# A two-layer mixture-of-experts trunk: full fp32 one-hot products, the router fed between two norms, the first token tile placed under the second

## The chip, the cores and the metric

The kernel runs on one core of one Trainium2 chip. The metric is the device time of one launch in microseconds (us), the median of several runs; less is better. The core's engines are named PE (TensorE, which multiplies matrices; PEld is its loading of weights), DVE (VectorE), ACT (ScalarE), POOL (GpSimd) and SP (SyncE, which here issues the weight transfers).

## The reference, cut to what matters

The input is 256 tokens of 1024 numbers, and there are two layers. In each layer `mod = silu(c) @ w_mod[l] + b_mod[l]` is split into six vectors of 1024: shift 1, scale 1, gate 1, shift 2, scale 2, gate 2 (`v` = 0 to 5 in the kernel).

```
h = layer_norm_plain(x) * (1 + sc1) + sh1
q, k, v, p = split(h @ w_in[l])
y = concat([attention(rope(q), rope(k), v), pool_mixer(p)]) @ w_out[l]
x = layer_norm_affine(alpha * x + g1 * y)
h = layer_norm_plain(x) * (1 + sc2) + sh2
scores = softmax(h @ w_router)
gates = top-2 experts inside the best of four groups, by scores + router_bias, weights normalised
y = sum over 16 experts e of gates[:, e] * (silu(h @ w_gate[e]) * (h @ w_up[e])) @ w_down[e]
x = layer_norm_affine(alpha * x + g2 * y)
```

Everything is float32. The weights are some 280 MB, and each is read once.

## The kernel before, in words

The tokens stand in two tiles of 128 (`t` = 0, 1). SP issues all weight transfers in one fixed order, the list `st` (class `Stream`), in pieces of 1 MB, into a ring of 21 buffers (`NS`); `st.allow(n)` says how many of them may hold weights, and `st.free` gives one back when PE has used it. The order of work on each engine is the order in which the code calls it; an engine does its instructions in that order.

A layer has these stages. The **entry** (`ready`, `enter`, `qk_mm`, the last loop of the file): the first scale and shift are multiplied out (`mod_mm`, `mod_fin`), the rows are normed, transposed, scaled and shifted, and multiplied with the query and key weights. The **mixer** (`mixer`): values, pooling, attention, and on DVE the sums over the weights of three other vectors (`mod_dve`, L361). The **routing**: `out_mm(t)` multiplies with `w_out` (L622), `norms_of(t)` adds the residual and does both norms on DVE, `turn(t)` transposes the normed rows (L653), `logits(t)` multiplies them with the router weights (L697), `exps(t)` finishes the softmax (L712 to L714), `router` chooses the experts for both tiles together on DVE (L782 to L810) and finds each token's place in its expert's batch of 64 slots (L816 to L824). `gate()` spreads gate 2 over the partitions (L347, L349). `warm(n)` are matrix products without use (L283), put where PE would stand idle. The **experts**: `onehot` writes a 0/1 matrix of token by slot, `gather(i)` multiplies the normed rows with it (L876), for four pairs of experts at a time (i = 0 and 4). Then for each of 8 pairs: `gate_up` (L918), `silu`, `act_t` (transposes, L941), `down` (L960), and `combine`, which adds the weighted rows back to their tokens through the transposed 0/1 matrix `STt` (L984).

In `gather` and `combine` a float32 operand is split into two of the type float32r: a rounded part and the rest (`xh`, `xl`; `oh`, `ol`). Each product is then made twice, once with each part:

```
for xs in (xh, xl):
    T.matmul(b, xs[:, t, k * 128:(k + 1) * 128], SX[i][t], start=(n == 0), stop=(n == 3))
```

DVE and ACT make the parts (L679, L725 to L727 for the rows; L973, L974 for the experts' results). Only the second half of the last pair's columns is combined by float32 products as they are (L980).

## Time and profile before

| | |
|---|---|
| time, median of 3 runs | 723.83 us (722.95 to 725.26) |
| time of the profiled execution | 724.93 us |
| its span, first to last instruction | 723.1 us |
| mean granted clock of PE | 0.986 of full speed |
| PE busy | 678.9 us, 94% of the span |
| DVE busy | 326.8 us, 45% |
| ACT busy | 124.8 us, 17% |
| moved by DMA | 280.37 MB, mean 388 GB/s |

The profile is of one execution. All its times count from the first instruction. A matrix product of float32 numbers leaves two MATMUL records, one of float32r or bfloat16 leaves one. A row of the timeline merges neighbours of one kind (x48 is 48 records), and what ended the idle time before it stands in brackets.

### The profile page before, as it was taken

What the parts mean: (1) busy time and instruction counts of PE and PEld (TensorE: products, weight loads), DVE (VectorE), ACT (ScalarE), POOL (GpSimd) and SP (SyncE); (2) the same over time, 40 slices, a digit from 0 to 9 for tenths busy, and PEclk for the clock granted to TensorE, in tenths of its full rate; (3) what the DMA queues carried; (4) which work ended last, traced back from release to release, by engine and by line L of the source; (5) the groups of instructions that cost most, each with busy time, mean ns of one, the idle gap of its engine ahead of it and who ended that gap; (6) DMA issues with size and microseconds to landing.
All of it is one profiled execution on the core that took longest, in us unless ns stands there. A gap on an engine that the chain in (4) does not pass through costs nothing. (4 is left out here: it accounts for less than half of the span.)

```text
span 723.1 us, 8334 instructions
## 1 busy us (share of the span) xinstructions
PE 678.9 (94%) x3213; PEld 316.8 (44%) x3218; DVE 326.8 (45%) x582; ACT 124.8 (17%) x268; POOL 49.7 (7%) x76
## 2 busy tenths in 40 slices
PE   5999899999999999989979999998999999998994
PEld 2447555553333533423324575555333344342331
DVE  4008897662332532413153966666323243241305
ACT  1011432130110210121002035213210011012100
POOL 5001501100000000000010051010000000000002
PEclk9999999999999999999989999999999999999998
DMA  9999999999999999999999999767699999999992
GB/s 307 366 384 409 408 409 420 373 421 392 424 420 420 422 421 421 420 416 418 395 406 392 409 410 406 310 272 301 282 420 422 421 424 419 420 422 418 418 395 77
DMA packets 61729, 280.37 MB, mean 388 GB/s; under 512 B 5008, under 2 KB 14264, under 8 KB 38632
## 3 DMA queue, kind: packets, MB, share of 16 engines
q1 hardware_dynamic: 61040, 279.20, 96.1%
q8 instruction: 30, 0.49, 0.3%
q10 hardware_dynamic: 312, 0.32, 0.1%
q0 software_dynamic: 320, 0.14, 0.1%
q14 instruction: 27, 0.22, 0.1%
HBM read 278.59 MB, written 1.05 MB: 387 GB/s over the span
## 5 line engine op out<-in xcount | busy, mean ns | idle before, releaser
L918 PE MATMUL ps<-wr 128*64 128x512 f32 x1024 | 226.1, 596 | 0.0
L918 PEld LDWEIGHTS ps<-wr 128*64 128x64 f32 x1024 | 73.5, 138 | 147.2 <-issue 142.3
L960 PE MATMUL ps<-wr,s 128*64 128x512 f32 x512 | 113.8, 595 | 3.7 <-DVE s L945 2.9
L960 PEld LDWEIGHTS ps<-wr,s 128*64 128x64 f32 x512 | 35.5, 137 | 72.0 <-issue 63.8
L970 DVE SCALAR_TENSOR_TENSOR s<-ps,gc,gb 128x512 f32<-128x512 f32 x32 | 24.0, 748 | 84.0 <-PE ps L960 84.0
L455 PE MATMUL ps<-wr,hT 128*128 128x512 f32 x128 | 57.0, 597 | 0.4 <-ACT hT L429 0.2
L361 DVE SCALAR_TENSOR_TENSOR wr<-wr,condT 128x1024 f32<-128x1024 f32 x42 | 55.8, 1329 | 2.3 <-DMA wr<-in_w_mod_dram 0.9
L622 PE MATMUL ps<-wr,hT 128*128 128x512 f32 (+1 forms) x160 | 55.7, 507 | 0.1
L389 POOL TENSOR_TENSOR rs<-rs,mhalf 128x1 f32<-128x1 f32 x16 | 13.2, 823 | 554.1 <-DVE rs L388 554.1
L935 DVE TENSOR_TENSOR s<-s,ps 128x512 f32<-128x512 f32 x16 | 11.0, 687 | 86.5 <-PE ps L918 86.5
L973 ACT CAST wr<-s 128x512 fp32r<-128x512 f32 x30 | 18.5, 618 | 164.7 <-PE ps L918 107.7
L974 DVE TENSOR_TENSOR wr<-s,wr 128x512 fp32r<-128x512 f32 x30 | 20.8, 692 | 55.6 <-ACT wr L973 55.6
L622 PEld LDWEIGHTS ps<-wr,hT 128*128 128x128 f32 x160 | 30.2, 190 | 23.8 <-issue 21.5
L455 PEld LDWEIGHTS ps<-wr,hT 128*128 128x128 f32 x128 | 23.6, 190 | 28.9 <-issue 27.1
L984 PE MATMUL ps<-wr,sT 128*128 128x512 f32 x120 | 33.6, 413 | 0.0
L578 PE MATMUL ps<-wr,hT 128*128 128x512 f32 x64 | 28.3, 595 | 0.0
L504 PE MATMUL ps<-hT,wr 128*128 128x256 f32 x128 | 28.1, 380 | 0.0
L984 PEld LDWEIGHTS ps<-wr,sT 128*128 128x128 f32 x120 | 20.9, 189 | 16.3 <-issue 13.0
L933 DVE SCALAR_TENSOR_TENSOR s<-s,ps 128x512 f32<-128x512 f32 x16 | 11.0, 685 | 36.7 <-ACT s L932 36.7
L504 PEld LDWEIGHTS ps<-hT,wr 128*128 128x128 f32 x128 | 24.2, 190 | 4.5 <-issue 1.3
L876 PE MATMUL ps<-s,xn 128*128 128x512 f32 x64 | 25.4, 398 | 0.3 <-DVE s L854 0.3
L996 DVE TENSOR_TENSOR xt<-xt,ps 128x512 f32<-128x512 f32 x40 | 25.2, 683 | 0.5
(240 smaller groups left out, 611.5 us busy)
## 6 DMA issues: line engine op xcount, KB each, us to landing
wr<-in_w_gate_dram SPq DMA_DIRECT2D x64, 1024.0 KB, 19.3
wr<-in_w_up_dram SPq DMA_DIRECT2D x60, 1024.0 KB, 19.3
wr<-in_w_down_dram SPq DMA_DIRECT2D x56, 1024.0 KB, 19.5
wr<-in_w_mod_dram SPq DMA_DIRECT2D x48, 1024.0 KB, 15.1
wr<-in_w_in_dram SPq DMA_DIRECT2D x16, 1024.0 KB, 15.1
wr<-in_w_out_dram SPq DMA_DIRECT2D x8, 1024.0 KB, 18.7
wr<-in_w_down_dram SPq DMA_DIRECT2D x12, 512.0 KB, 11.1
wr<-in_w_up_dram SPq DMA_DIRECT2D x8, 512.0 KB, 17.4
```

The source lines that it names most:

```text
L361: V.scalar_tensor_tensor(acc, w[:, kk], condT[:, k, 0:1], acc, op0=OP.mult, op1=OP.add)
L455: T.matmul(pq[t][n], hT[:, k, t * 128:(t + 1) * 128], w[:, kk, n * 512:(n + 1) * 512], start=(k == 0), stop=(k == 7))
L504: T.matmul(pp[g // 2][:, (g % 2) * 256:(g % 2) * 256 + 256], w[:, kk, g * 128:(g + 1) * 128], hT[:, k, :], start=(k == 0 and g % 2 == 0), ...
L578: T.matmul(pv[t], hT[:, k, t * 128:(t + 1) * 128], w[:, kk, :], start=(k == 0), stop=(k == 7))
L622: T.matmul(py[t][-1][:, 0:c1 - c0], catT[:, k, t * 128:(t + 1) * 128], w[:, kk, n * 512 + c0:n * 512 + c1], start=(q == 2 and kk == 0), st ...
L876: T.matmul(b, xs[:, t, k * 128:(k + 1) * 128], SX[i][t], start=(n == 0), stop=(n == 3))
L918: T.matmul(bs[nm][64 * j:64 * j + 64, :], XE[i][k // 4][:, k % 4, c0:c0 + 64], st.get((nm, l, 2 * i + j, q))[:, k - k0, :], start=(k == 0) ...
L960: T.matmul(bo[n][64 * j:64 * j + 64, :], AT[i][:, k, 64 * j:64 * j + 64], st.get(("d", l, 2 * i + j, q))[:, k - k0, (n - n0) * 512:(n - n0 ...
L970: V.scalar_tensor_tensor(o, bo[n], GC[i], g2[:, c0], op0=OP.mult, op1=OP.mult)
L974: V.tensor_sub(ol[:, c0], o, oh[:, c0].bitcast(F))
L984: T.matmul(b, STt[i][:, t * 128:(t + 1) * 128], o[:, n * 512:(n + 1) * 512], start=(start and j == 0), stop=(stop and j == 1), skip_group_ ...
L996: V.tensor_add(b if i == NPAIR - 3 else xt[:, t, c0], xt[:, t, c0], b)
```

## The change

Five things are changed.

1. `gather` and `combine` use float32 operands as they are, and each product is made once. The parts `xh`, `xl`, `oh`, `ol` and the instructions that make them go. The experts' results stand in the buffer `hT` instead of a slot of the ring for each pair, and two of the limits of `st.allow` are one higher.
2. The scale and shift of the second layer's entry (vectors 1 and 0) were multiplied out by vector: vector 1 in the first layer's routing, with its `mod_fin` in the second pair, vector 0 at the entry. Now it is by halves of the columns, both vectors at once (`mod1`): half 0 at the entry, half 1 between the query and key products, which go in four parts. The weights come in that order, behind the experts' weights.
3. `turn(t)` takes the rows between the two norms. The mean and the spread of the second norm are put in at the logits (two more instructions on DVE), from sums over the router weights that 16 products make (L749 in the new file, 8 before).
4. `out_mm` is cut in parts. The logits and the choice of experts for tile 0 (`route(0)`) and its places (`place(0)`) come between the parts for tile 1, and the gather's products with tile 0 for four of eight row blocks behind them. Tile 1 follows by itself: `turn(1)`, logits, `gate()`, softmax, `route(1)`, `place(1)`, then 12 products of the gather. Tile 1's second norm goes to ACT. Of the 10 products of `warm` in layer 0's routing and the 17 in layer 1's, two each stay.
5. In layer 0 the transposed queries are copied by ACT instead of DVE (L528).

```diff
-        if l + 1 < DEPTH:
-            add_mod(l + 1, 1)
         for i in range(NPAIR):
             add_pair(l, i)
         if l + 1 < DEPTH:
-            add_mod(l + 1, 0)
+            for q in range(4):
+                if q % 2 == 0:
+                    add_mod1(q // 2)
+                add_qk(l + 1, q)
...
+    def mod1(h):
+
+        acc = ps()
+        for k in range(8):
+            for v in range(2):
+                j = 2 * v + k % 2
+                T.matmul(acc[32 * j:32 * j + 32, :], condT[:, k, :], st.get(("m1", h, v, k // 4))[:, k % 4, :],
+                         start=(k < 2), stop=(k > 5))
+            if k % 4 == 3:
+                for v in range(2):
+                    st.free(("m1", h, v, k // 4))
...
+
             ready(0)
-            qk_mm(0)
+            enter(l, 0, 0, hT, xn)()
+            qk_mm(0, (0, 1))
+            part = mod1(1)
             ready(1)
+            enter(l, 1, 0, hT, xn)()
+            mod1_fin(1, part)
+            fins = [enter(l, 0, 1, hT, xn)]
+            qk_mm(1, (0, 1))
+            fins.append(enter(l, 1, 1, hT, xn))
+            for fin in fins:
+                fin()
+            qk_mm(0, (2, 3))
...
-                (A.copy if n else V.tensor_copy)(dst[:, :, t * 128:(t + 1) * 128], b.rearrange("p (c s) -> p c s", c=4))
+                (A.copy if n or not l else V.tensor_copy)(dst[:, :, t * 128:(t + 1) * 128], b.rearrange("p (c s) -> p c s", c=4))
...
+        def place(t):
+
+            pb = ps()
+            if t:
+                T.matmul(pb[:, 0:16], ones, M[:, 0], start=True, stop=False)
+            T.matmul(pb[:, 0:16], tri, M[:, t], start=not t, stop=True)
+            V.scalar_tensor_tensor(posm[:, t], M[:, t], -OFF, pb[:, 0:16], op0=OP.mult, op1=OP.add)
+            return onehot_t(posm, 0, t)
...
+        exps(0, logit_mm(0))
+        route(0)
+        out_mm(1, 1)
+        residual(1, 1)
+        out_mm(1, 2, (2, 3))
+        S0 = [place(0)]
+        out_mm(1, 2, (0, 1))
+        residual(1, 2)
+        first_norm(1)
+
+        gb0 = [ps() for _ in range(4)]
+        for k in range(4):
+            T.matmul(gb0[k], xn2[:, 0, k * 128:(k + 1) * 128], S0[0], start=True, stop=False)
...
         turn(1)
         logits(1)
-        exps(1)
-        return xh, xl, (mx, ex, sm), gate
+        pl = logit_mm(1)
+        gate()
+        st2[1] = mv, rs = stats(xt[:, 1])
+        exps(1, pl)
+
+        nb = tn([1], "r_nb")
+        V.scalar_tensor_tensor(nb, mv[:, 0:1], -1.0, rs, op0=OP.mult, op1=OP.mult)
+        o, i = in_rows(1)
+        A.activation(o, i, AF.Identity, scale=rs, bias=nb)
+        route(1)
+        warm(2)
+        S0.append(place(1))
...
+        def part_mm(b, i, k, t):
+            T.matmul(b, X[:, t, k * 128:(k + 1) * 128], SX[i][t], start=(t == 0), stop=(t == 1))
+
         def gather(i):
 
             halves = [slot().rearrange("p (k s) -> p k s", k=4) for _ in range(2)]
+            for j in range(4):
+                XE[i + j] = halves
             for k in range(8):
                 b = ps()
-                n = 0
                 for t in range(2):
-                    for xs in (xh, xl):
-                        T.matmul(b, xs[:, t, k * 128:(k + 1) * 128], SX[i][t], start=(n == 0), stop=(n == 3))
-                        n += 1
-                o = halves[k // 4][:, k % 4]
-                if k % 2:
-                    V.tensor_scalar(o, b, sc2[:, k:k + 1], sh2[:, k:k + 1], op0=OP.mult, op1=OP.add)
-                else:
-                    A.activation(o, b, AF.Identity, scale=sc2[:, k:k + 1], bias=sh2[:, k:k + 1])
+                    part_mm(b, i, k, t)
+                modulate(b, halves[k // 4][:, k % 4], k)
+
+        def gather_first():
+
+            halves = [slot().rearrange("p (k s) -> p k s", k=4) for _ in range(2)]
             for j in range(4):
-                XE[i + j] = halves
+                XE[j] = halves
+            bs = dict(enumerate(gb0))
+            for k in (4, 5):
+                bs[k] = ps()
+                part_mm(bs[k], 0, k, 0)
+            for k in range(8):
+                if k > 5:
+                    bs[k] = ps()
+                    part_mm(bs[k], 0, k, 0)
+                part_mm(bs[k], 0, k, 1)
+                modulate(bs[k], halves[k // 4][:, k % 4], k)
...
-                so = s1p.tile([128, S], FR, name="sT", bufs=3)
+                so = s1p.tile([128, S], F, name="sT", bufs=3)
...
-            w = slot(FR)
-            O[i] = oh, ol = w[:, 0:D], w[:, D:2 * D]
+            O[i] = ob[:, i % 2]
...
-                    o = s2()
                     c0 = slice(n * 512, (n + 1) * 512)
-                    V.scalar_tensor_tensor(o, bo[n], GC[i], g2[:, c0], op0=OP.mult, op1=OP.mult)
-                    if last and n:
-                        break
-                    A.copy(oh[:, c0], o)
-                    V.tensor_sub(ol[:, c0], o, oh[:, c0].bitcast(F))
+                    V.scalar_tensor_tensor(O[i][:, c0], bo[n], GC[i], gb[l, 5][:, c0], op0=OP.mult, op1=OP.mult)
...
         def combine_mm(i, t, n, b, start=True, stop=True):
-            for j, o in enumerate(O[i]):
-                T.matmul(b, STt[i][:, t * 128:(t + 1) * 128], o[:, n * 512:(n + 1) * 512],
-                         start=(start and j == 0), stop=(stop and j == 1), skip_group_check=not start)
+            T.matmul(b, STt[i][:, t * 128:(t + 1) * 128], O[i][:, n * 512:(n + 1) * 512],
+                     start=start, stop=stop, skip_group_check=not start)
...
-            if i == 1 and l + 1 < DEPTH:
-                mod_fin(l + 1, 1)
...
-            mod_mm(l, 0)
+            part0 = mod1(0)
```

PE in layer 0's routing. Before, from the second tile's product with `w_out` (L622; L297 is `mod_mm` for vector 5 and for the next layer's vector 1, L653 `turn`, L697 `logits`, L712 the logits' sum, L347 the first half of `gate()`):

```order
L622 MATMUL ps<-wr,hT 128x512 x8
L622 MATMUL ps<-wr,hT 128x256 x16
L688 MATMUL ps<-col_843,wr__105 32x1 x8
L653 MATMUL ps<-ident,wr 128x128 x8
L697 MATMUL ps<-wr,wrp 32x128 x8
L297 MATMUL ps<-wr,condT 32x512 x32
L712 MATMUL ps<-sel_157,s_909 128x16
L653 MATMUL ps<-ident,wr 128x128 x8
L697 MATMUL ps<-wr,wrp 32x128 x8
L712 MATMUL ps<-sel_157,s_909 128x16
L347 MATMUL ps<-s_962,selm 128x512
```

The same place now, from the first tile's logits (L769) on (L664 is `out_mm`, L812 `place`, L828 the first part of the gather, L301 `mod_mm`, L697 `turn`, L738 `logits`, L376 `gate()`); ahead of it stand the first eight products of `out_mm` for tile 1, `turn(0)` and `logits(0)`:

```order
L769 MATMUL ps<-sel_157,s_877 128x16
L664 MATMUL ps<-wr,hT 128x256 x12
L812 LDWEIGHTS tri
L812 MATMUL ps<-r_M,tri 128x16
L664 MATMUL ps<-wr,hT 128x256 x4
L828 MATMUL ps<-s_982,xn 128x512 x4
L301 MATMUL ps<-wr,condT 32x512 x16
L697 MATMUL ps<-ident,xt 128x128 x8
L738 MATMUL ps<-wr,wrp 32x128 x8
L769 MATMUL ps<-sel_157,s_877 128x16
L376 MATMUL ps<-s_1035,selm 128x512
```

The first tile's transposes, logits and place have moved into `out_mm` of the second, four gather products stand ahead of `mod_mm`, and half of `mod_mm` is gone from here.

ACT at the second tile's softmax. Before (L654 copies of `turn`, L699 of `logits`, L714 the softmax's exponentials, L349 the copies of `gate()`, L882 the gather's scaling):

```order
L654 COPY wr<-ps 128x4x128 x2
L699 ACTIVATE s_909<-ps,rbias 128x128
L714 ACTIVATE r_ex,r_sm<-ps,r_mx 128x16
L349 COPY gb<-ps 128x512 x2
L882 ACTIVATE wr<-ps,col_843,col_694 128x512 x4
```

Now (L698, L740, L378, L777 and L938 are the same five, L841 is the second norm of tile 1):

```order
L698 COPY wr<-ps 128x4x128 x2
L740 COPY s_877<-ps 128x128
L378 COPY gb<-ps 128x512 x2
L777 ACTIVATE r_ex,r_sm<-r_lg,r_mx 128x16
L841 ACTIVATE xn<-xt,r_nb,rs 128x1024
```

The exponentials, on which `route(1)` waits, have moved behind the two copies of `gate()`.

PE at the second layer's entry. Before (L437 `enter`, L455 `qk_mm`, L504 the pooling branch's product):

```order
L437 MATMUL ps<-ident,xn 128x128 x8
L455 MATMUL ps<-wr,hT 128x512 x16
L437 MATMUL ps<-ident,xn 128x128 x8
L455 MATMUL ps<-wr,hT 128x512 x16
L504 MATMUL ps<-hT,wr 128x256 x32
```

Now (L465 `enter`, L488 `qk_mm`, L339 `mod1(1)`, L351 `mod1_fin(1)`, L548 the pooling branch):

```order
L465 MATMUL ps<-ident,xn 128x128 x4
L488 MATMUL ps<-wr,hT 128x512 x8
L339 MATMUL ps<-wr,condT 32x512 x16
L465 MATMUL ps<-ident,xn 128x128 x4
L351 MATMUL ps<-ident,s_5206 128x128 x4
L465 MATMUL ps<-ident,xn 128x128 x4
L488 MATMUL ps<-wr,hT 128x512 x8
L465 MATMUL ps<-ident,xn 128x128 x4
L488 MATMUL ps<-wr,hT 128x512 x16
L548 MATMUL ps<-hT,wr 128x256 x32
```

The first query and key products need half as many transposes ahead of them, and the 16 products of `mod1(1)` with their transposes stand among them.

## Rows read from the trace of the kernel before

**Rows 1.** Who waited for whom, PE for DMA: us in total, times, longest

```profile
PE ps L297 <- DMA wr<-in_w_mod_dram: 3.6, 2, 2.5
```

**Rows 2.** Busy time by window: layer 1's routing, layer 1's experts

```profile
core 0: us, PE busy (x) PEld busy (x) DVE busy (x) ACT busy (x) POOL busy (x), PEclk, DMA share, GB/s
468.00:507.00 39.00, 35.80 (x210) 21.41 (x209) 26.14 (x55) 9.63 (x20) 2.62 (x3) 1.00 0.71 285
507.00:713.00 206.00, 200.12 (x917) 78.11 (x916) 67.89 (x121) 25.34 (x42) 0.22 (x1) 1.00 0.96 393
```

**Rows 3.** Timeline of PE: a full `gate_up`, layer 1's last half: start, us

```profile
159.34 13.95 PE L918 MATMUL ps<-wr 128*64 128x512 f32 x64
...
682.89 8.01 PE L918 MATMUL ps<-wr 128*64 128x512 f32 x32
```

**Rows 4.** Groups by line and form: busy us, mean ns of a record

```profile
L622 PE MATMUL ps<-wr,hT 128*128 128x512 f32 x96 | 41.9, 592 | 0.1
...
L980 PE MATMUL ps<-s,sT 128*128 128x512 f32 x8 | 3.8, 595 | 0.0
```

**Rows 5.** Timeline of PE: layer 0's first gather, then its second (32 products)

```profile
152.89 0.39 PE L876 MATMUL ps<-s,xn 128*128 128x512 f32 x1
...
159.02 0.39 PE L876 MATMUL ps<-s,hT 128*128 128x512 f32 x1
...
247.77 0.47 PE L876 MATMUL ps<-s,xn 128*128 128x512 f32 x1
...
255.16 0.60 PE L894 MATMUL ps<-ident,s 128*128 128x128 f32 x4
```

**Rows 6.** Timeline of PE, second pair of layer 0

```profile
196.52 2.14 PE L984 MATMUL ps<-wr,sT 128*128 128x512 f32 x8
198.50 0.63 PE L941 MATMUL ps<-ident,s 128*128 128x128 f32 x4
200.35 0.66 PE L335 MATMUL ps<-ident,s 128*128 128x128 f32 x4 [1.22 <-ACT s L330]
```

**Rows 7.** Timeline of PE, layer 0's routing

```profile
119.33 13.94 PE L622 MATMUL ps<-wr,hT 128*128 128x512 f32 x48
...
142.76 1.07 PE L653 MATMUL ps<-ident,wr 128*128 128x128 f32 x8
...
145.72 2.18 PE L347 MATMUL ps<-s,selm 128*128 128x512 f32 x4
```

**Rows 8.** Timeline of PE, the second layer's entry

```profile
366.12 1.92 PE L297 MATMUL ps<-wr,condT 128*32 128x512 f32 x16
...
372.74 1.93 PE L297 MATMUL ps<-wr,condT 128*32 128x512 f32 x8 [2.49 <-DMA wr<-in_w_mod_dram]
...
380.43 14.00 PE L455 MATMUL ps<-wr,hT 128*128 128x512 f32 x32
...
409.25 13.98 PE L504 MATMUL ps<-hT,wr 128*128 128x256 f32 x64
```

**Rows 9.** Timeline of DVE, layer 0's routing

```profile
136.77 1.28 DVE L399 SCALAR_TENSOR_TENSOR xt<-wr,rs 128x1024 f32<-128x1024 f32 x1 [0.44 <-POOL rs L389]
...
146.64 0.17 DVE L782 RECIPROCAL r_sm<-r_sm 128x2 f32<-128x2 f32 x1 [0.43 <-ACT r_ex L714]
...
150.23 0.19 DVE L810 SCALAR_TENSOR_TENSOR r_M<-r_rk,r_fg 128x32 bf16<-128x32 f32 x1
```

**Rows 10.** Timeline of ACT, second copy of `gate()` in layer 0

```profile
148.15 0.58 ACT L349 COPY gb<-ps 128x512 f32<-128x512 f32 x1 [0.49 <-PE ps L348]
```

**Rows 11.** Timeline of all engines, layer 0's attention

```profile
73.79 1.27 DVE L528 COPY wr<-ps 128x512 f32<-128x512 f32 x2
74.62 2.08 PE L534 MATMUL ps<-wr 64*128 64x128 f32 x16 [3.48 <-DVE wr L528]
...
76.77 0.70 DVE L554 TENSOR_TENSOR ps<-ps,mask 128x512 f32<-128x512 f32 x1 [1.70 <-PE ps L534]
```

**Rows 12.** Busy time by window, columns as in rows 2: PE's slow stretches

```profile
74.60:78.00 3.40, 3.38 (x24) 3.24 (x26) 1.67 (x3) 0.00 (x0) 3.16 (x6) 0.50 1.03 411
372.70:379.50 6.80, 6.76 (x26) 2.74 (x26) 2.44 (x7) 0.58 (x1) 0.97 (x1) 0.58 1.02 405
```

More of the change, by code (lines that the diff above doesn't have):

```diff
@@ L10 @@
 BF = mybir.dt.bfloat16
-FR = mybir.dt.float32r
 I32 = mybir.dt.int32
@@ L109, in add_mod01, with add_mod1 @@
             st.add(("m01", h, v), w[:, :, v * D + h * 256:v * D + (h + 1) * 256])
+    def add_mod1(h):
+        w = w_mod[1].rearrange("(p k) n -> p k n", k=8)
+        for v in (1, 0):
+            for q in range(2):
+                st.add(("m1", h, v, q), w[:, 4 * q:4 * q + 4, v * D + h * 512:v * D + (h + 1) * 512])
     def add_qk(l, q):
@@ new lines, in mixer, with tn @@
+        A.activation(rsum[:, 0:1], bb[:, 0:1], AF.Copy, scale=-1.0)
+        A.copy(rsum[:, 1:2], bb[:, 1:2])
+        logits(0)
+        cb = ps()
+        for i in range(2):
+            T.matmul(cb[:, i * 16:i * 16 + 16], rsum[:, i:i + 1].to_broadcast([128, 128]), sel16[:, 0:NE],
+                     start=True, stop=True)
+        crow = const.tile([128, 2, 16], F, name="crow", bufs=1)
+        A.copy(crow, cb[:, 0:32].rearrange("p (i e) -> p i e", i=2))
+        def tn(shape, name, dt=F):
+            return tiny.tile([128] + shape, dt, name=name, bufs=1)
@@ L1150, in ready @@
                 b = tiny.tile([128, 2, 6], F, name="bn")
-                if not t:
-                    own.append(ends(0))
+                own.append(ends(t))
                 for n in range(2):
@@ L1158, in ready @@
                 if not t:
-                    mod_fin(l, 0)
+                    mod1_fin(0, part0)
                     warm(8)
-                    own.append(ends(1))
-                V.tensor_scalar(xn[:, t], xt[:, t], mv[:, 0:1], rs, op0=OP.subtract, op1=OP.mult)
-                enter(l, t, hT, xn)
-        xh, xl, mes, gate = mixer(l, hT, xn, ready)
-        r = router(l, mes, gate)
-        ends, norm, norm_aside = experts(l, xh, xl, *r)
+                for n in range(2):
+                    V.tensor_scalar(xn[:, t, n * 512:(n + 1) * 512], xt[:, t, n * 512:(n + 1) * 512],
+                                    mv[:, 0:1], rs, op0=OP.subtract, op1=OP.mult)
+        ends, norm, norm_aside = experts(l, *mixer(l, hT, xn, ready))
     rest = xt[:, 1, 512:D]
```

307 lines of the change are left out of this document (148 added, 159 removed).

## The prediction

> **What bounds the kernel now.** I read first who waited for whom on PE. Its only wait of any size for a transfer comes to 3.6 us, at one place [rows 1]; the other weights are there when PE comes to them. Then the windows: over layer 1's experts PE is busy for 200.12 of 206 us at full clock, DMA moves 393 GB/s, and DVE is busy for a third [rows 2]. In that layer's routing DMA falls to 285 GB/s, since the ring is full and PE, busy 35.8 of 39 us there, has not come to the experts. So DMA is nearly always at work only because it runs ahead, and it has slack to run ahead with. In one place it is nearly the bound as well: in the last pair 32 records take 8.01 us [rows 3] where the 64 records of a full `gate_up` take 13.95 [rows 3], or 7.0 for half of it, so that some 1.0 us is lost to late weights there. The reader is to see a PE whose work, laid end to end, is the time, with DMA close behind it. What the change adds to PE counts in full; what it takes from DVE and ACT counts only where PE waits for them.
>
> **One product in full fp32 against two of the parts.** A float32 product of 128x512 costs 41.9 / 48 = 0.87 us, as two records belong to one product; the shape with `STt` as weights gives 3.8 / 4 = 0.95, its end included [rows 4]. A float32r product costs (159.02 - 152.89) / 27 = 0.227 us, as the two rows are the first and the last of 28 in a run [rows 5]. Two parts cost 0.455, the whole 0.87: the edit halves the count and makes each nearly four times as dear.
> - The second gather takes 255.16 - 247.77 = 7.4 us now [rows 5], and 16 x 0.87 = 13.9 then: +6.5.
> - A pair's `combine` takes 198.50 - 196.52 = 2.0 us [rows 6], and 4 x 0.87 = 3.5 then: +1.5, in seven pairs of a layer +10.5. The last pair has four split products (1.0) that become two (1.7): +0.7.
> - DVE and ACT lose the making of the parts. In the experts nobody waits for it: PE makes 200 of 206 us. Worth nothing.
>
> Together +17.7 in each layer's experts. In layer 0 the transposes of `mod_fin` for vector 1 leave the second pair, with their idle 1.22 us and about 0.5 of work [rows 6]: -1.7, so **+16.0**. In layer 1 the late weights of the last pair (1.0) can't be late any more: DMA needs as long as before, PE longer: **+16.7**. I keep 15 to 19 for each.
>
> The Trainium skill, FP8 and Floating Point Precision, section TensorE Precision Notes, says that true FP32 takes four passes through the array and that the reduced form reads once. The trace agrees in kind: 0.87 / 0.227 is 3.8, in two records instead of four. By four full passes a product would cost 0.91, and the sum below would be some 5 us more; I keep the measured 0.87.
>
> **The routing, from the first product of `out_mm` for tile 1 to the first pair.** It takes 159.34 - 119.33 = 40.0 us in layer 0 [rows 3, 7] and 39.0 in layer 1 [rows 2]. PE's new order, step by step: 8 products of `out_mm`, 7.0; `turn(0)`, `logits(0)` and their sum as now, 145.72 - 142.76 = 3.0 [rows 7], and 0.4 for the sums over the router weights; 16 products of half the width, 7.0; four of the gather, 3.5; `mod_mm` for vector 5, 32 records at 1.92 for 16 with the last one's end [rows 8], 3.6; `turn(1)`, `logits(1)`, sum, 3.0. That is 27.5. Two things run beside it. Tile 0's softmax and choice must be done within the next 12 products of `out_mm` (5.3 us): it needs some 4.3, so there is one us to spare. Tile 1's first norm ends 4.8 us after its last product (138.05 against 119.33 + 13.94) [rows 7, 9], and PE has 7.1 us of other work then: no wait. The norm that `turn` waited for is taken off PE's path here, and the time goes to the work put in its place.
>
> Behind the second tile's logits it is a chain that nothing covers. The exponentials now stand behind the copies of `gate()` on ACT, and the second copy ends 148.73 - 145.72 = 3.0 us after `gate()` starts on PE [rows 7, 10]. Then the exponentials, about 0.5. Then `route(1)`: for both tiles the choice takes 150.42 - 146.64 = 3.8 us [rows 9]; for one tile it is two operations shorter and each has half the width, but these are operations of 0.2 us that hardly shrink; I take 3.3 (2.5 to 3.8). Then `place(1)`, 0.2. Of the 12 gather products left, two cover the making of the 0/1 matrix; all 12 take 10.4. Sum 27.5 + 3.0 + 0.5 + 3.3 + 0.2 + 10.4 = 44.9: **+4.9** in layer 0 and **+5.9** in layer 1 (from +3 to +8 each).
>
> **The clock.** In that chain PE has `gate()` and two `warm` products, some 2.9 us, and then stands for about 3.9 us until the choice is there. In layer 0's attention it stood for 3.48 us [rows 11], and the granted clock was 0.50 for the 3.4 us behind it, the level of 1.2 GHz [rows 12]; that costs 1.7 us. Nothing in the new order shortens the wait, so I add 1.7 in each layer: **+3.4** (0 if the clock holds).
>
> **The second layer's entry.** From `mod_mm` to the first query product it takes 380.43 - 366.12 = 14.3 us [rows 8]. In it lie the 3.6 us of waits for weights [rows 1], and 6.8 us at a clock of 0.58 [rows 12], of which 2.9 are lost. Both go: four pieces of 1 MB are no longer ahead of the experts' weights (at 410 GB/s some 10 us), and PE comes later by all that was added. 14.3 - 3.6 - 2.9 = 7.8: -6.5 (-3.6 if DVE's norm is what is late next). The stretch from there to the pooling product, 28.8 us [rows 8], takes up the 16 products of `mod1(1)` (3.6) and ten or so transposes more (1.3): +4.9. Together **-1.6** (-4 to +2). `mod_mm` for vector 1, which left the routing, is paid here.
>
> **Layer 0's attention.** PE waits 3.48 us for DVE's copies [rows 11], which go to ACT. DVE, free at 73.79, began the softmax at 76.77 because its products came late; now it can begin at once. From there DVE's sums set the pace up to `out_mm`, so I take **-3.0** (-1.3, the copies alone, to -5.2, wait and slow clock).
>
> The other edits (limits of the ring, the buffer of the experts' results, halves in `ready`) only move work of DVE or transfers under PE's work, and are costed at nothing; if the ring should starve PE that is a rival below.
>
> **Sum.** -3.0 + 4.9 + 16.0 - 1.6 + 5.9 + 16.7 + 3.4 = +42.3 us. The profiled execution took 724.93, so it would take 767.2; against the median of 723.83 that is **766**, 5.8% slower.
>
> **Rivals.**
> - *The fp32 products cost no more than the two parts* (0.455). In the two layers 116 new ones lie on PE's path (16 + 28 + 2 + 12 in each): 116 x 0.415 = 48 us less, 718 us, faster than before. It decides below 0.50 a product (42.3 / 116 off 0.87). For it: only that one operand of each holds just zeros and ones; against it L980, the same shape in fp32, at 0.95. Chance 0.03.
> - *The extra work is hidden by DMA.* If the experts are set by the transfers, their +32.7 vanish: 733. For it: DMA at 393 GB/s and the late weights at the end. Against it: no other wait for weights. 0.05.
> - *The chain is lighter*: the clock holds and the choice for one tile takes 2.5 us less with what stands before it: 766 - 3.4 - 5 = 757.5. The rows for short idle times don't rule it out. 0.18.
> - *A new wait*: tile 0's choice misses its one us, so that `place(0)` holds up PE in front of the second half of the last product; or the experts' weights come late, as the ring fills earlier in layer 1 and DMA has 285 GB/s there already. At 3 us for a miss in each layer and 8 for the ring: 772 to 780. 0.12.
>
> **How the numbers follow.** The likeliest case, the sum, has 0.60; with its bounds it spans 758 to 774. The remaining 0.02 is what I did not see. To leave out no more than 2 in 10, I reach down to 749 over the lighter chain and up to 777 over most of the new waits. The two cases at the bottom lie outside. What the runs can tell from no change is about 0.3%, 2.2 us; only the first rival ends on the other side of it: faster 0.03, the same 0.01, slower 0.96.
>
> **What would show it.** The gather's and combine's MATMUL records at 0.43 us a step, two for each product: 14 us for the second gather, 3.5 us for a combine. No wait of PE for `w_mod` at layer 1's entry. An idle of PE of about 4 us before `place(1)`, with a clock of 0.5 behind it. Layer 0's first pair at about 161 to 163 us, layer 1's at about 530. DMA slower on average, with a deeper dip in layer 1. The prediction is wrong if a product comes at under 0.5 us, or if PE waits for weights inside the experts.

## The result

The changed kernel takes 767.64 us (median of 4 runs, 766.92 to 770.67). The kernel before, run beside it, takes 724.24 us (722.95 to 725.26). The ratio is 1.0608, with a 95% interval of 1.0574 to 1.0642: 43.4 us slower. The profiled execution took 768.11 us, its span is 766.3 us, the mean granted clock 0.985, PE is busy for 726.1 us (95%; 678.9 before), DVE for 309.8 and ACT for 109.3, and DMA moves 366 GB/s on average (388 before).

Who PE waits for in the changed kernel: us in total, times, longest.

```profile
PE ps L812 <- DVE r_M L804: 7.4, 2, 3.7
PE ps L287 <- DVE ones L224: 6.6, 1, 6.6
PE ps L437 <- PEq L1132: 3.9, 2, 2.0
```

The wait for `w_mod` of [rows 1] is gone. A new one heads the list: 3.7 us in each layer, at `place(1)` (L812), for the choice of experts. The wait at the start (L287) is as before; the third line is the stop at a branch, `past()`, which comes to 4.1 us in the kernel before.

The timeline of PE in layer 0, from the end of the attention to the first pair. It answers to [rows 7, 9].

```profile
95.52 1.13 PE L401 MATMUL ps<-ident,wr 128*128 128x128 f32 x8 [2.35 <-DVE wr L390]
...
98.48 13.90 PE L664 MATMUL ps<-wr,hT 128*128 128x512 f32 x32
...
116.95 7.03 PE L664 MATMUL ps<-wr,hT 128*128 128x512 f32 x16
...
131.94 0.17 PE L812 MATMUL ps<-r_M,tri 128*128 128x16 bf16 x1
...
143.56 0.40 PE L769 MATMUL ps<-sel,s 128*128 128x16 f32 x2 [0.39 <-ACT s L740]
...
150.34 0.17 PE L812 MATMUL ps<-r_M,tri 128*128 128x16 bf16 x1 [3.70 <-DVE r_M L804]
...
150.42 13.18 PE L941 MATMUL ps<-s,xn 128*128 128x512 f32 x24
163.54 2.80 PE L1002 MATMUL ps<-wr 128*64 128x512 f32 x12
```

The routing is the stretch from 116.95 to 163.54: 46.6 us instead of 40.0. `place(0)` at 131.94 waits for nothing. `place(1)` waits 3.70, and the 24 records behind it take 13.18 us, 0.55 each, where 32 of the same kind take 13.90 below, 0.43 each. The granted clock is 0.50, the level of 1.2 GHz, from 150.42 to 155.50 and 1.00 from 156.50 on. The first row is what became of the attention's gain: PE now waits 2.35 us for DVE's sums, and `out_mm` begins at 98.48 us; it began at 100.86 us before.

Three places of the experts on PE: a combine, the second gather, and, in each layer, the half of a `gate_up` behind `past()`, the branch on the experts' counts that stands in the middle of the seventh pair's `gate_up`. They answer to [rows 3, 5, 6].

```profile
200.72 3.70 PE L1061 MATMUL ps<-hT,sT 128*128 128x512 f32 x8
204.25 0.63 PE L1025 MATMUL ps<-ident,s 128*128 128x128 f32 x4
...
255.17 13.90 PE L941 MATMUL ps<-s,xn 128*128 128x512 f32 x32
268.91 0.60 PE L978 MATMUL ps<-ident,s 128*128 128x128 f32 x4
...
336.65 7.09 PE L1002 MATMUL ps<-wr 128*64 128x512 f32 x32
...
705.32 8.75 PE L1002 MATMUL ps<-wr 128*64 128x512 f32 x32
```

A combine takes 204.25 - 200.72 = 3.53 us, two records for each of 4 products; the second gather takes 268.91 - 255.17 = 13.7.

The second layer's entry on PE, which answers to [rows 8].

```profile
385.10 3.64 PE L339 MATMUL ps<-wr,condT 128*32 128x512 f32 x32
...
392.87 7.13 PE L488 MATMUL ps<-wr,hT 128*128 128x512 f32 x16 [0.55 <-ACT hT L474]
...
426.31 13.98 PE L548 MATMUL ps<-hT,wr 128*128 128x256 f32 x64
```

No transfer is waited for. From `mod1(0)` to the first query product it takes 7.8 us (14.3 before), from there to the pooling product 33.4 (28.8 before).

Layer 1's routing and experts as windows, with the columns of [rows 2].

```profile
485.14:532.04 46.90, 42.25 (x215) 22.06 (x214) 25.15 (x69) 11.41 (x22) 2.62 (x3) 0.93 0.53 215
532.04:755.47 223.43, 218.49 (x917) 78.43 (x916) 59.81 (x104) 15.17 (x26) 0.00 (x0) 0.99 0.88 362
```

Layer 1's routing is 46.9 us long where it was 39.0, its experts 223.4 where they were 205.25 (to the end of the last combine in both). DMA falls to 215 GB/s in the routing, deeper than the 285 of [rows 2].

### The profile page after: what moved, and what is told of

The parts are those of the page before. It is cut to its first block, busy times and chain, and to the rows that moved or that the text cites. A ratio compares the mean times of both kernels' runs of the same rounds, so it can differ in the third digit from the quotient of the medians.

```text
span 766.3 us, 8305 instructions
## 1 busy us (share of the span) xinstructions
PE 726.1 (95%) x3235; PEld 317.2 (41%) x3235; DVE 309.8 (40%) x580; ACT 109.3 (14%) x244; POOL 50.6 (7%) x76
## 5 line engine op out<-in xcount | busy, mean ns | idle before, releaser
L1052 DVE SCALAR_TENSOR_TENSOR hT<-ps,gc,gb 128x512 f32<-128x512 f32 x32 | 24.0, 751 | 89.5 <-PE ps L1043 87.7
L1061 PE MATMUL ps<-hT,sT 128*128 128x512 f32 x128 | 60.2, 605 | 0.0
L488 PE MATMUL ps<-wr,hT 128*128 128x512 f32 x128 | 57.1, 596 | 0.6 <-ACT hT L474 0.5
L664 PE MATMUL ps<-wr,hT 128*128 128x512 f32 (+1 forms) x160 | 56.4, 509 | 0.0
L941 PE MATMUL ps<-s,xn 128*128 128x512 f32 x112 | 54.3, 647 | 0.0
L664 PEld LDWEIGHTS ps<-wr,hT 128*128 128x128 f32 x160 | 29.9, 190 | 23.0 <-issue 20.3
L1016 ACT ACTIVATE s<-ps 128x512 f32<-128x512 f32 x16 | 9.6, 602 | 188.9 <-PE ps L1002 188.9
L1061 PEld LDWEIGHTS ps<-hT,sT 128*128 128x128 f32 x128 | 22.6, 190 | 33.1 <-issue 31.2
L488 PEld LDWEIGHTS ps<-wr,hT 128*128 128x128 f32 x128 | 23.5, 190 | 28.4 <-issue 26.6
L941 PEld LDWEIGHTS ps<-s,xn 128*128 128x128 f32 x112 | 23.0, 209 | 28.2 <-issue 27.3
L1073 DVE TENSOR_TENSOR xt<-xt,ps 128x512 f32<-128x512 f32 x40 | 27.5, 688 | 10.3 <-PE ps L1061 10.3
L936 DVE TENSOR_SCALAR wr<-ps,col,col 128x512 f32<-128x512 f32 x16 | 13.0, 809 | 41.9 <-PE ps L941 39.2
L622 PE MATMUL ps<-wr,hT 128*128 128x512 f32 x64 | 28.3, 595 | 0.0
L548 PE MATMUL ps<-hT,wr 128*128 128x256 f32 x128 | 28.1, 380 | 0.0
```

Of the source, the lines that this page charges most:

```text
L488: T.matmul(pq[t][n], hT[:, k, t * 128:(t + 1) * 128], w[:, kk, n * 512:(n + 1) * 512], start=(k == 0), stop=(k == 7))
L548: T.matmul(pp[g // 2][:, (g % 2) * 256:(g % 2) * 256 + 256], w[:, kk, g * 128:(g + 1) * 128], hT[:, k, :], start=(k == 0 and g % 2 == 0), ...
L622: T.matmul(pv[t], hT[:, k, t * 128:(t + 1) * 128], w[:, kk, :], start=(k == 0), stop=(k == 7))
L664: T.matmul(py[t][j][:, 0:b - a], catT[:, k, t * 128:(t + 1) * 128], w[:, kk, a:b], start=(q == 2 and kk == 0), stop=(q == 1 and kk == 1))
L936: V.tensor_scalar(o, b, sc2[:, k:k + 1], sh2[:, k:k + 1], op0=OP.mult, op1=OP.add)
L941: T.matmul(b, X[:, t, k * 128:(k + 1) * 128], SX[i][t], start=(t == 0), stop=(t == 1))
```

## The experiments

All times are medians beside runs of the kernel before on the same chip (medians 722.6 to 723.6 us). Where a run is compared with the changed kernel, the two medians come from different chips; the changed kernel stood beside 724.24, so that such a difference is 1.3 to 1.6 us smaller when each is taken beside its own runs of the kernel before. Three questions: are the float32 products the whole loss, what does the new order do by itself, and do the waits that the prediction named cost what it said?

**1. The products alone.** The order of before; `gather` and `combine` take float32 operands whole.

```diff
-                    for xs in (xh, xl):
-                        T.matmul(b, xs[:, t, k * 128:(k + 1) * 128], SX[i][t], start=(n == 0), stop=(n == 3))
-                        n += 1
+                    T.matmul(b, X[:, t, k * 128:(k + 1) * 128], SX[i][t], start=(t == 0), stop=(t == 1))
...
-            for j, o in enumerate(O[i]):
-                T.matmul(b, STt[i][:, t * 128:(t + 1) * 128], o[:, n * 512:(n + 1) * 512],
-                         start=(start and j == 0), stop=(stop and j == 1), skip_group_check=not start)
+            T.matmul(b, STt[i][:, t * 128:(t + 1) * 128], O[i][:, n * 512:(n + 1) * 512],
+                     start=start, stop=stop, skip_group_check=not start)
```

> The kernel before in its old order, with full float32 products in gather and combine and nothing else of the change. Theory (PE pays 0.87 us for one float32 product against 0.455 for the two parts, in full): per layer +17.7 in the experts and 16 x 0.87 - 32 x 0.227 = +6.6 in the first gather, less the waits and the slow clock at the second layer's entry (3.6 + 2.9) and the late weights at the end (1.0), which go since PE comes later: 724.2 + 48.6 - 7.5 = 765. Rival (the experts are set by DMA and hide PE's work; the new order is what costs): 730 to 740.

Measured: 766.09 us, ratio 1.0596 (1.0567 to 1.0625). The products alone lose 43.1 us, the whole change 43.4. With the old entry and the slow products PE waits for no `w_mod` at layer 1's entry: from there to the pooling product it takes 425.95 - 388.59 = 37.4 us, where the kernel before needs 43.1.

**2. The order alone.** The changed kernel with the products in two float32r parts, and the parts' buffers as before. One thing of the new order goes with it: tile 1's second norm is on DVE again, with the making of its parts.

```diff
-            T.matmul(gb0[k], xn2[:, 0, k * 128:(k + 1) * 128], S0[0], start=True, stop=False)
+            T.matmul(gb0[k], xh[:, 0, k * 128:(k + 1) * 128], S0[0], start=True, stop=False)
...
-            T.matmul(b, X[:, t, k * 128:(k + 1) * 128], SX[i][t], start=(t == 0), stop=(t == 1))
+            for j in js:
+                T.matmul(b, X[j][:, t, k * 128:(k + 1) * 128], SX[i][t], start=(t == 0 and j == 0), stop=(t == 1 and j == 1))
```

> The changed kernel with both gathers and combine made from float32r parts again, all else of the new order kept (the second tile's normed rows and parts are made by DVE ahead of the choice). Theory of the products: per layer -17.7 in the experts, -6.6 in the first gather: 767.6 - 48.6 = 719, some 1 to 4 us more if weights come late again at the end. The idle time before the second tile's choice (3.7 us) and the slow clock behind it stay. Rival (the new order costs the time): above 740.

Measured: 736.75 us, ratio 1.0198 (1.0167 to 1.0229). Missed by 18 us: the order alone does not gain 4 us, it loses 13.8; the rival's 740 isn't reached either. The two halves of the change don't add up either: 43.1 + 13.8 = 56.9, and together they cost 43.4. PE's timeline in this run, at layer 1's entry and at its attention:

```profile
367.49 5.08 PE L340 MATMUL ps<-wr,condT 128*32 128x512 f32 x32 [5.11 <-DMA wr<-in_w_mod_dram]
...
431.55 1.65 PE L572 MATMUL ps<-ident,xn 128*128 128x128 f32 x8 [3.94 <-DVE xn L887]
```

The first operation of the rotation on DVE:

```profile
426.11 2.08 DVE L882 TENSOR_TENSOR s<-xn,cs 128x128 f32<-128x128 f32 x1
```

PE waits 5.11 us for the weights of `mod1`, and later 3.94 us for DVE's rotation of the queries, whose first operation takes 2.08 us (0.28 in the kernel before; run 11 says why). Layer 1's mixer is 66.7 us long where it was 58.8, so that 7.8 us of the loss lie there. Some 1.7 more lie in layer 1's routing, where PE waits 4.45 us for `place(1)` with DVE's norm in the chain. DMA is behind. The windows from 120 to 180 us, layer 0's routing and the first pair, show where it fell behind; the last column is GB/s. First the kernel before:

```profile
120.00:140.00 20.00, 19.63 (x131) 11.49 (x133) 13.84 (x27) 3.23 (x6) 2.12 (x3) 1.00 0.99 397
140.00:160.00 20.00, 17.92 (x111) 10.21 (x103) 12.21 (x29) 7.04 (x14) 0.50 (x1) 1.00 0.99 403
160.00:180.00 20.00, 18.86 (x90) 6.63 (x88) 5.73 (x18) 2.18 (x4) 0.00 (x0) 1.00 0.97 394
```

Then the order alone:

```profile
120.00:140.00 20.00, 19.50 (x149) 12.50 (x147) 15.48 (x39) 4.17 (x12) 1.85 (x2) 1.00 0.82 333
140.00:160.00 20.00, 14.90 (x71) 9.08 (x74) 13.00 (x38) 7.44 (x13) 0.55 (x1) 0.91 0.77 322
160.00:180.00 20.00, 18.86 (x92) 6.74 (x90) 4.49 (x11) 0.97 (x2) 0.00 (x0) 1.00 0.93 377
```

The shares of 0.77 to 0.93 are a DMA that stands still, as I read it because the ring is full: 20 us x (64 + 81 + 17 GB/s) = 3.2 MB, about 8 us at 410 GB/s. What was emptying the ring there before? In the kernel before, the 4 MB of vector 1 are used up in the middle of layer 0's routing. The next four runs follow this.

**3. The order alone, with the entry of before.**

```diff
-            for q in range(4):
-                if q % 2 == 0:
-                    add_mod1(q // 2)
-                add_qk(l + 1, q)
+            add_mod(l + 1, 0)
...
         route(1)
-        warm(2)
+        if l + 1 < DEPTH:
+            mod_mm(l + 1, 1)
+        else:
+            warm(2)
```

> The new order of the routing with the products in two parts, as in the run of the order alone (736.75 us), but with the entry of before: vector 1's 4 MB stand between vector 5 and the experts again, its 16 products stand before place(1) in layer 0 in place of two fills, vector 0 is multiplied out at the entry. Theory: the order alone lost its time because these 4 MB no longer empty the ring in the routing (DMA 333, 322 and 377 GB/s over 120 to 180 us where before had 397, 403 and 394; that is 3.2 MB, 8 us of transfer), so that the weights come late at layer 1's entry, and DVE's sums with them, and the rotation of the queries. Then DMA moves some 390 GB/s there again, PE waits no more than 3 us for w_mod, the entry and the mixer take the 102 us of before and not 115, and the time is 722 us (719 to 726). Rival: it is the routing's order that starves the ring (tile 0 by itself, the slots held longer): then the entry waits as before the edit and the time stays at 732 or more.

Measured: 729.47 us, ratio 1.0074 (1.0055 to 1.0094). The loss beside the kernel before falls from 13.8 to 5.9 us. Layer 1's mixer takes 58.8 us again (66.7 in run 2, 58.83 in the kernel before). But the time lies between the two expectations: DMA still makes only 304 GB/s from 120 to 140 us (421 and 418 after that), so a part of the loss seems to belong to the new order of the routing itself, in which `out_mm` for tile 1 and the products of vector 5, and with them their slots, come later. By the stages of the two traces, 2.4 us more than before are spent in layer 1's routing (41.4 us; PE waits 4.45 for `place(1)`) and 4.0 more in layer 0's experts.

**4. The new entry alone, in the kernel before.**

```diff
-        if l + 1 < DEPTH:
-            mod_mm(l + 1, 1)
...
-            mod_mm(l, 0)
+            part0 = mod1(0)
```

> The kernel before with the new entry alone: vectors 1 and 0 by halves behind the experts' weights, nothing of vector 1 in layer 0's routing. Theory (the 4 MB are what empties the ring in the routing): DMA loses some 3 MB in layer 0's routing, PE waits about 5 us for w_mod at the entry and the rotation of layer 1's queries is late by some 5 us; 732 us (728 to 737), slower than before. Rival (my prediction's own sum for the entry, -1.6, and the products of vector 1 out of the routing): 719 to 723.

Measured: 738.00 us, ratio 1.0197 (1.0176 to 1.0218): 14.4 us slower, one us above the theory's range and far from the rival's. Layer 0's routing is only 1.0 us shorter without the 16 products (159.33 - 120.36 = 39.0 us), as PE waits 2.31 us for DVE's norm in their place. DMA makes 373, 285 and 326 GB/s in the three windows. The lost time shows in two places. One is layer 1's mixer: PE waits for the rotation as in run 2, and the stretch from the pooling product to `out_mm` for tile 1 takes 67.1 us (58.8). The other is `past()` in layer 0. PE at both, then the branch itself on PE's queue of weight loads and on SP, and the queue that brings instructions, from 320 to 322 us:

```profile
308.39 7.04 PE L960 MATMUL ps<-wr 128*64 128x512 f32 x32
322.90 1.89 PE L438 MATMUL ps<-rowz,selz 128*128 128x512 bf16 x4 [7.48 <-issue]
324.72 7.96 PE L960 MATMUL ps<-wr 128*64 128x512 f32 x32
...
434.47 1.06 PE L571 MATMUL ps<-ident,xn 128*128 128x128 f32 x8 [3.92 <-DVE xn L787]
```

```profile
L1100 PEldq COMPARE_BRANCH  x1: 6277/6277/6277, 311.0 to 311.0; - x1
...
L1100 SPq COMPARE_BRANCH  x1: 50/50/50, 330.7 to 330.7; - x1
```

```profile
q8 instruction: 1, 0.02, 3.5%
```

PE stands for 7.48 us (1.92 in the kernel before), and the trace names no releaser. It does not wait for SP: SP comes to the same branch at 330.7 us, 8 us after PE went on (at 331.0 in the kernel before, 12 us after). What goes with PE's stop is the loading of instructions. At all 28 passages of `past()` in the traces of this case a packet of 16 KB on queue q8 lands shortly before PE goes on: in 26 of them, with stops of 1.9 to 2.8 us, 1.6 to 1.8 us ahead. In the two long stops, here and in run 5, PE's branch ends as in the others (317.26 here, 1.4 us behind its packet), and PE goes on 1.3 to 1.4 us after a second packet, which lands here at 321.61. That the stop is a wait for code is read from these times; no run tested it. So the 5.6 us more at `past()` say nothing of the 4 MB. Run 5 shows what they cost.

**5. Vector 1 late, and nothing by halves.** The kernel before, with vector 1's weights behind the experts' and its products at the entry.

```diff
-        if l + 1 < DEPTH:
-            add_mod(l + 1, 1)
         for i in range(NPAIR):
             add_pair(l, i)
         if l + 1 < DEPTH:
+            add_mod(l + 1, 1)
             add_mod(l + 1, 0)
...
+            mod_mm(l, 1)
             mod_mm(l, 0)
```

> The kernel before with one thing moved: vector 1's 4 MB stand behind the experts' weights instead of ahead of them, and its 16 products and its sums stand at layer 1's entry ahead of vector 0's, by vector as before; nothing by halves, the query and key products in one piece. Theory (PE's use of these 4 MB in the routing is what empties the ring there, and without it DMA stands still for some 10 us and never gets that time back before layer 1's mixer): DMA loses some 4 MB between 120 and 180 us, PE waits some 10 us more at past() or at the entry, 735 us (731 to 740), as with the entry by halves (738.0). Rival: what cost the entry alone its 14 us was the order by halves (DVE's sums and the rotation late behind query products in four parts); then only PE's 16 products and their sums are added to the entry, and the time is 726 to 729.

Measured: 734.82 us, ratio 1.0166 (1.0132 to 1.02). The theory's time holds: a move of 4 MB and 16 products costs 12.2 us, with the old query and key products. DMA makes 388, 269 and 311 GB/s in the three windows, 4.5 MB less than before. PE at the entry:

```profile
382.32 1.94 PE L296 MATMUL ps<-wr,condT 128*32 128x512 f32 x8 [0.60 <-DMA wr<-in_w_mod_dram]
...
418.77 13.98 PE L503 MATMUL ps<-hT,wr 128*128 128x256 f32 x64
```

The last piece of `w_mod` is used at 382.32 us, and PE waits for it; before, it was 372.74 [rows 8]. That is 9.6 us later, about what 4.5 MB take at 410 GB/s (11 us), and the pooling product comes 9.5 us later. PE stands for 7.7 us at `past()` here too; as DMA moves 417 GB/s from 200 to 360 us all the same and PE still waits for `w_mod` behind it, I take that stop to be hidden under the late transfers. The mixer takes 58.8 us, as before: without the halves the rotation isn't late.

**6. The old entry in the changed kernel.** The edit of run 3, with float32 products.

```diff
-            part0 = mod1(0)
+            mod_mm(l, 0)
...
-        warm(2)
+        if l + 1 < DEPTH:
+            mod_mm(l + 1, 1)
+        else:
+            warm(2)
```

> The changed kernel with the entry of before: vector 1's 4 MB ahead of the experts, its 16 products before place(1) in layer 0 in place of two fills, its sums in the second pair, vector 0 at the entry, query and key products in one piece. In the changed kernel no weight is late at the entry, so the sum is PE's work alone: the 16 products stand in the chain's idle time, which keeps the clock there (-2.6 in layer 0); their transposes go back to the second pair (+1.7); the stretch from the entry to the pooling product is 7.8 + 28.8 and no more 7.8 + 33.4 (-4.6). 762 us (760 to 765), if DMA keeps its cover there. Rival: my prediction's -1.6 for the entry by halves stands for something that the old entry would lose (its 4 MB more at the first query product make PE wait again): 766 or more.

Measured: 761.86 us, ratio 1.0547 (1.0511 to 1.0583), 5.8 us under the changed kernel. PE's timeline:

```profile
385.63 3.64 PE L303 MATMUL ps<-wr,condT 128*32 128x512 f32 x32
...
394.15 14.00 PE L488 MATMUL ps<-wr,hT 128*128 128x512 f32 x32
...
422.98 2.32 PE L538 MATMUL ps<-hT,wr 128*128 128x256 f32 x10
```

From the entry to the pooling product it is 37.4 us; with the halves it is 41.2, without a wait for weights in either. So the entry by halves is no gain where DMA has cover; it is 3.9 us of PE's time more at this place, while the old order has its 16 products for vector 1 in the idle time of the routing's chain.

**7. More products to fill the chain.** The changed kernel; it tests the clock.

```diff
-        warm(2)
+        warm(18)
```

> The changed kernel with 18 products without use instead of 2 while PE waits for the second tile's choice. Theory (after an idle time of 3.7 us the clock falls to half, 1.7 us lost in each layer): the 24 gather records behind the choice take 10.5 us instead of 13.2, no stretch of half clock there, 764. Rival (those records are slow because the 0/1 matrix or the rows come late): they still take 13 us, time as it was, 767.6.

Measured: 763.79 us, ratio 1.0558 (1.0526 to 1.059), 3.9 us under the changed kernel. PE's timeline:

```profile
150.63 0.17 PE L812 MATMUL ps<-r_M,tri 128*128 128x16 bf16 x1 [0.24 <-DVE r_M L804]
...
150.71 10.55 PE L941 MATMUL ps<-s,xn 128*128 128x512 f32 x24
```

`place(1)` comes no earlier (150.34 before the edit), but PE did not stand, and the 24 records take 10.55 us instead of 13.18. The window over them has a granted clock of 1.00, where it is 0.80 in the changed kernel.

**8. The exponentials ahead of `gate()`.** The changed kernel; it tests the chain on ACT.

```diff
-        gate()
         st2[1] = mv, rs = stats(xt[:, 1])
         exps(1, pl)
+        gate()
```

> The changed kernel with the exponentials of the second tile called ahead of gate(), so that they stand ahead of its two copies on ACT. Theory (the chain of the choice waits for those copies, 2.4 us): PE's idle time before the second tile's place falls from 3.7 to about 1.3 us in each layer, and with so short an idle time the clock holds: 767.6 - 2 x 2.4 - 2 x 1.7 = 759. If the clock falls all the same, 763. Rival (the choice waits for DVE, not ACT): no change.

Measured: 758.92 us, ratio 1.0494 (1.0452 to 1.0535), 8.7 us under the changed kernel. PE's timeline:

```profile
145.38 0.40 PE L769 MATMUL ps<-sel,s 128*128 128x16 f32 x2 [0.39 <-ACT s L740]
...
150.24 0.17 PE L812 MATMUL ps<-r_M,tri 128*128 128x16 bf16 x1 [1.78 <-DVE r_M L804]
...
150.32 10.55 PE L941 MATMUL ps<-s,xn 128*128 128x512 f32 x24
```

From the logits' sum (L769) to `place(1)` it takes 4.86 us; it took 150.34 - 143.56 = 6.78. That is 1.9 us a layer, and as PE stands for 1.78 us only, the clock holds and gives another 2.6.

**9. The copy by ACT alone**, in the kernel before.

```diff
-                (A.copy if n else V.tensor_copy)(dst[:, :, t * 128:(t + 1) * 128], b.rearrange("p (c s) -> p c s", c=4))
+                (A.copy if n or not l else V.tensor_copy)(dst[:, :, t * 128:(t + 1) * 128], b.rearrange("p (c s) -> p c s", c=4))
```

> The kernel before with ACT for the copies of layer 0's transposed queries, nothing else. Theory: the first product of layer 0's out_mm comes 2.4 us earlier, as in the changed kernel, and nothing gives it back: 720.6 us (720 to 721.5). Rival: the weights, which come at the rate of DMA, give it back at layer 1's entry: 723.

Measured: 722.11 us, ratio 0.9986 (0.997 to 1.0003). Not settled: the gain may be anything from 2 us to nothing. In its trace the first pair begins 1.8 us earlier than before (157.50), and PE's waits for `w_mod` at the entry come to 4.1 us (3.6 in [rows 1]).

**10. The best order that these runs point to.** Run 3 with the exponentials first and 18 fills in layer 1.

```diff
-            warm(2)
+            warm(18)
```

> e7 with two more edits in the routing: the exponentials of tile 1 stand ahead of gate()'s copies on ACT, and 18 fills instead of two stand before place(1) in layer 1 (in layer 0 vector 1's products stand there). It computes what the reference asks, with the products in two parts. If DMA was what the order lost its time to, PE's shorter routing counts: 717 us (713 to 720), faster than both kernels. Rival: the transfers set the time from here on, and PE waits for weights at the entry or in the last pairs what it saves in the routing: 722 to 724.

Measured: 728.09 us, ratio 1.0064 (1.005 to 1.0078). The rival held, and more: it is slower than before. Layer 0's first pair begins 2.6 us earlier (156.72), the entry 1.0 us later (367.12). The profile's waits of PE for DMA in this run:

```profile
PE ps L304 <- DMA wr<-in_w_mod_dram: 3.3, 3, 1.5
...
PE ps L1000 <- DMA wr<-in_w_gate_dram: 1.6, 2, 1.2
```

They stand in layer 0's last pair and at the entry. In the last pair the half of a `gate_up` with the two waits takes 9.9 us instead of 7.0, and that is most of what PE saved ahead of it; the waits at the entry are no longer than before (3.6 us). In layer 1 the new routing takes 39.1 us, no less than the old 39.0.

**11. The combine in parts**, in the changed kernel: the edit of run 1, reversed for `combine` only, with the making of the parts on DVE and ACT and their slots in the ring.

```diff
-            T.matmul(b, STt[i][:, t * 128:(t + 1) * 128], O[i][:, n * 512:(n + 1) * 512],
-                     start=start, stop=stop, skip_group_check=not start)
+            for j, o in enumerate(O[i]):
+                T.matmul(b, STt[i][:, t * 128:(t + 1) * 128], o[:, n * 512:(n + 1) * 512],
+                         start=(start and j == 0), stop=(stop and j == 1), skip_group_check=not start)
```

> The changed kernel with the combine's products in two parts again (the gather stays in float32). By PE's work alone 2 x (7 x 1.5 + 0.7) = 22.4 us go, which gives 745 us (743 to 747). Rival: DMA, which had 17 us of cover at layer 1's entry, becomes the bound there again, as in the run of the order alone: PE waits for w_mod at the entry and DVE's rotation is late, 749 to 753.

Measured: 755.58 us, ratio 1.0451 (1.0415 to 1.0486). By the prediction's terms 22.4 us of PE's work went (PE is busy for 20.7 us less), and 12.1 us of time: less than either expectation had it, on the rival's side. Layer 1's mixer takes 67.2 us here; it takes 58.8 in the changed kernel. DVE in it, and POOL at the same time:

```profile
434.44 2.08 DVE L879 TENSOR_TENSOR s<-xn,cs 128x128 f32<-128x128 f32 x1
```

```profile
433.70 2.67 POOL L888 TENSOR_TENSOR wr<-wr 128x1084 f32<-128x1084 f32 x1 [8.62 <-ACT wr L558]
```

DVE's sums wait for late pieces of `w_mod`, so that the rotation behind them starts when POOL is at its pooling sums. An operation of 0.28 us takes 2.08 and ends at 436.52, where POOL's ends at 436.37. The Trainium skill, SBUF — State Buffer, section Who interferes with whom, says that a VectorE instruction with two inputs in SBUF and a GpSimd instruction that reads SBUF exclude each other, and that the later one blocks until the first is done. The trace agrees, and runs 2 and 4 have the same row (2.08 us, beside a POOL sum). In the changed kernel the rotation is done at 437.4 us and POOL starts at 441.0.

**12. The rotation between DVE's sums**, in run 11.

```diff
             mod_dve(l, 2, acc[2])
-            mod_dve(l, 4, acc[4])
         rope(qk)
+        if l:
+            mod_dve(l, 4, acc[4])
```

> The run of the split combine (755.58 us) with one line moved: in layer 1 DVE's rotation of queries and keys stands between its sums for vectors 2 and 4, not behind both. Theory: 8.3 of the 10 us that run lost against 745 lie in layer 1's mixer, since DVE's sums wait for late w_mod pieces, the rotation behind them is late, and at its later hour it runs beside the pooling sums on POOL, where one of its operations takes 2.08 us and not 0.28. Moved ahead it is done at about 427 us, before POOL starts; PE's wait of 3.9 us for the rotation and the half clock behind it go, a wait for the sums of vector 4 of some 2 us may come: 750 us (748 to 752). Rival: the rotation is not what sets it, PE then waits as long for the sums that end later: 755.

Measured: 751.74 us, ratio 1.0402 (1.0373 to 1.0431), 3.8 us under run 11. DVE, then PE:

```profile
423.40 0.28 DVE L880 TENSOR_TENSOR s<-xn,cs 128x128 f32<-128x128 f32 x1
```

```profile
438.98 1.94 PE L402 MATMUL ps<-ident,wr 128*128 128x128 f32 x8 [4.76 <-DVE wr L391]
```

The rotation takes 0.28 us an operation again and nobody waits for it; PE waits 4.76 us for the sums of vector 4, more than the 2 expected. Now those sums run beside POOL's: seven operations of L391 take 11.97 us, where the same seven take 9.5 in run 11. The collision moved on with the lateness, and a part of it is still paid.

## Why the prediction was right, and where its reasons were not

| term | predicted | measured in the trace |
|---|---|---|
| layer 0's attention | -3.0 | -2.4 |
| routing, layer 0, with its share of the clock | +4.9 + 1.7 | +6.6 |
| experts, layer 0 | +16.0 | +14.8 |
| entry of layer 1 | -1.6 | -1.9 |
| routing, layer 1, with its share of the clock | +5.9 + 1.7 | +7.9 |
| experts, layer 1 | +16.7 | +18.2 |
| sum | +42.3 | +43.2 |

The half of a `gate_up` behind `past()` in the kernel before, in layer 0 and in layer 1, to set beside 336.65 and 705.32 of the changed kernel:

```profile
319.87 8.78 PE L918 MATMUL ps<-wr 128*64 128x512 f32 x32
...
666.30 7.09 PE L918 MATMUL ps<-wr 128*64 128x512 f32 x32
```

- *The products.* A gather product costs 13.7 / 16 = 0.86 us, a combine's 3.53 / 4 = 0.88: 0.87 was right, and both rivals that lived on it (0.455 a product, and the work hidden by DMA) are out by run 1. The two layers' experts differ from their terms by -1.2 and +1.5 for one reason: the slow half `gate_up` behind `past()` stood in layer 0 before (8.78 us against 7.09) and stands in layer 1 now (8.75), 1.7 us each way. Neither the prediction nor a run says in which layer it falls; that the two cancel in the sum is luck.
- *The routing.* The lengths came out, though two things in them were mis-sized: the wait before `place(1)` was put at 3.9 us (3.70), and the clock at 1.7 a layer, while the 24 records lose 2.6, since it stays at 0.50 for some 5 us of them and not 3.4. That layer 0's sum is right to 0.1 us is luck: PE's work up to `gate()` and the chain behind it came out some 0.9 us shorter than their terms. Runs 7 and 8 show both causes on the chip: the clock costs 2.6 to 3.9 us in all, the exponentials behind `gate()`'s copies 1.9 a layer more. `place(0)` kept 0.7 of its spare microsecond (the choice is done at 131.25, PE comes at 131.94). Layer 0's first pair begins at 163.54, a little behind the 161 to 163 of the forecast.
- *The attention.* The wait went, but DVE's sums of `w_mod` end later than PE comes (2.35 us), as the term's last sentence said; -2.4 of the -3.0.
- *The entry.* The number was right, and a reason for it was wrong. The prediction let the late weights be cured twice over: "four pieces of 1 MB are no longer ahead of the experts' weights", some 10 us, and PE comes later. Runs 4 and 5 refute the first. The 4 MB were no burden in the routing: their use there emptied the ring while PE had nothing else to take from it, and without it DMA stands still for as long as it would have needed for them. In the kernel before, that edit alone costs 14.4 us, and the move without the halves 12.2. Only the second reason held: the float32 products make PE so late that DMA has caught up, and run 1 shows it with the old entry too. Run 6 shows what is left of the edit then: PE's work, 3.9 us more than the old entry.
- *What the sum could not show.* Run 1 (+43.1), run 2 (+13.8) and the whole (+43.4) don't add, since the cover that the slow products give hides the order's loss. A sum of terms over one trace was right here only because the largest term was there to hide the error of a small one, and that is luck. The other way round, run 11 took 22.4 us of work away and got 12.1: the cover went with it.

Left open: 5.9 us of the order alone are still lost in run 3. DMA's dip from 120 to 140 us, PE's waits for weights in layer 0's last pair and the longer routing of layer 1 go with them; run 10, which mends the routing, gets back 1.4, and no run set `out_mm`'s slots free earlier. What sets the length of PE's stop at `past()` is open as well. No version ran faster than the kernel before by more than its interval; run 9 is the nearest.

## What to carry to other kernels

When DMA runs ahead through a ring, as here, a piece of work that consumes weights while the other consumers stand can be worth more than its place in the order shows: here, moving its 4 MB later didn't relieve DMA, it stopped it. Before costing such a move, compare GB/s in the windows around the old place and ask which `free` lets SP go on there. And test the parts of a change apart, since a slow part can hide what a fast part breaks. When two engines go on at the same moment, look where each stands in its own order before calling one the cause of the other.

## What the runs showed of the hardware

- Behind 3.7 us without work PE's granted clock was 0.50 (1.2 GHz) over the first 5.1 us of the gather, 0.80 on average over its 13.1; behind a wait of 1.78 us, or with 18 bfloat16 products in the gap, it was full in the same place.
- A DVE operation on two SBUF operands took 2.08 us instead of 0.28 beside a POOL sum, and ended 0.15 us after it.
- At a branch PE stood for 1.9 to 2.8 us in 26 of 28 passages and went on 1.6 to 1.8 us after a packet of 16 KB had landed on the instruction queue; in the other two it stood for 7.5 and 7.7 us, and went on 1.3 to 1.4 us after a second one.
